# A hybrid decoder layer on one core: transposes of the normed rows move to the score banks, their inverse root comes from a square root, the last row blocks rank earlier, and one product gets its own bank

## Chip, core and metric

The kernel runs on one core of one Trainium2 chip. The metric is device microseconds for one execution. Times before the change: 1425.96, 1429.08 and 1431.47 us, median 1429.08 us. Engines are named as in the profile: PE (TensorE matmuls), PEld (its weight loads), DVE (VectorE), ACT (ScalarE), POOL (GpSimd), SP (SyncE, which issues most DMAs).

## The reference, cut to what matters

One layer over 1024 rows of 1024 columns, in float32:

```
proj = rms_norm(h, norm1_w) @ w_in
o_a  = gated delta rule, 4 heads      (scan over the rows)
o_b  = differential attention, 4 heads (two softmax maps per head)
h    = h + concat(o_a, o_b) @ w_out
u    = causal_dwconv3(rms_norm(h, norm2_w) @ w_up)      2 x 2816 columns: gate, up
h    = h + (silu(gate) * up) @ w_down
rms_norm(x, w) = x * rsqrt(mean(x*x) + 1e-6) * w
```

The change touches the passage from the attention to the third line from below: the output projection's second half, the second rms_norm, and the first products with w_up.

## The kernel before, in words

Every large product is made of three fp32r matmuls (high x high, high x low, low x high), so each operand is split into a high and a low part: ACT writes the high one, DVE or POOL the difference.

**Order of the work.** The kernel is written in the Tile framework: a list scheduler puts each engine's instructions in order when the program is built, by rank in the program. `part(name)` moves what it encloses ahead by `PRI[name]` places (lines 36 to 38). Each engine then runs its list strictly in order on the chip. Tiles come from rings: `g` (16 slots of 128x1024), `c` (4), `w` (5), `l` (2), `j` (2), and a new tile waits until the slot's last user is done.

**PSUM.** There are eight banks of 128x512. During the attention, pool `pq` has two banks of tag `G` (`psG`) and two of tag `t` (`sm`). Pool `pS2` (`psS`) has two tiles of two banks each, which hold the attention scores. After the attention both pools close (line 1201) and `pf[0]` and `pf[1]` take over, four banks each: `pf[0]` lies over `pq`'s four, `pf[1]` over the four score banks. `bank(i, s)` (line 1205) takes a bank of `pf[i % 2]`.

**The last head and the row blocks.** The 1024 rows are eight blocks of 128, and the last head's attention goes through them downwards, block 7 to block 0: scores and Exp in `attn1` (line 884; Exp in line 913), transposes `paT` and value products `pao` in `attn2` (line 924). `wout_b` (line 1107) follows block by block, in two steps:

- step 1 (`wb1`): load the rows into `hrow` (ring `c`), transpose the block's mixed heads into `trm` (`mix_T`, line 1048, one G bank), split it into `mhl` (lines 1054, 1055; ring `c`), 24 products into two `pwo` banks (lines 383 to 385), add them to `hrow` (line 1123), store it.
- step 2 (`wb2`): `rms_rows` (line 270) squares the row block with a sum on ACT (line 273, writing a fresh `g` tile `u`), takes the inverse root with `rsqrt_ss` (nine small DVE instructions, lines 193 to 198, the last six being three Newton rounds), and scales (line 276). `norm_T` (line 241) transposes `u` into two `sm` banks `tr` (line 246). `combine` (line 1069) reads them.

`combine` prepares a fast (Strassen-like) 2x2 block product: blocks 7 to 4 are split (lines 1085 to 1087). For blocks 3 to 0 ACT and DVE form `t1`, `t2`, `t3` and the splits of B22 and T2 (lines 1095 to 1104, line 1101 being the last read of the `tr` banks), POOL forms `t4` (line 1105).

**The first w_up products.** `up_early` (line 1246), for column blocks 0 and 1, computes two products that need only blocks 7 to 4 ("11" and "21", 24 matmuls each) into one bank `pe` of `pf[1]` (line 1254). Its weights hold four of the five `w` slots until they are done. `mv_split` (line 1211) splits T1, T3 and T4. `up(j)` (line 1261) makes the weight sums on POOL (lines 1270 to 1273), splits them (line 202 for rx, ry, rz) and runs five products of 12 matmuls in the order T2, T1, T3, 22, T4 (lines 1230 to 1232), in banks `pa` and `pc` of `pf[j % 2]`; for j from 2 on also "11" and "21". `rsqrt_act` (line 260) already exists: it is what the first stage of the kernel uses for its own norm, with Sqrt on ACT (line 264), then a reciprocal and one Newton round on DVE (lines 265 to 268).

Of the kernel before, what the change touches and what calls it, by code (L numbers as in the profile page):

```python
# [34 lines left out]

PRI = dict(dprep=1000, dscan=930, dinv=200, dout=100, dproj=100, dz1=100, qk0=370, v0=400,
           d_dec=0, d_k=-25, d_q=0, d_nat=50, d_sc=800, d_v=0, d_w=-430, qkn=970, qks=25, a2o=0,
           prep0=160, early_w=300, early=0, attn1=0, attn2=0, attn3=25, prep=-25, fill=0, wa=0, wb1=0, wb2=25, ffn=110)
FS = [2, 1, 2, 3, 2, 2, 2, 2]
PP0, PP1 = 4, 2  # L40
PRE_K = {5: 1, 6: 0}
# [17 lines left out]
def hybrid_layer(ctx, tc, x, positions, norm1_w, w_in, dn_conv_w, dn_a_log, dn_dt_bias,  # L59
# [60 lines left out]
    def psG(s="pG"):  # L120
        return pq.tile([P, 512], F32, tag="G", name=nm(s), bufs=2)
# [118 lines left out]

    def norm_T(src, ps_fn):
        pss = []
        for q in range(2):
            ps = ps_fn("tr")
            for k in range(4):
                PE.transpose(ps[:, k * P:(k + 1) * P], src[:, (4 * q + k) * P:(4 * q + k + 1) * P], ident)
            pss.append(ps)
        return pss
# [21 lines left out]
    def rms_rows(src, wrow, dst, junk, rsq=rsqrt_ss):  # L270

        ss = small("ss", 1, 4)
        S.activation(junk, src, AF.Square, accum_out=ss)
        rs = small("rs", 1, 4)
        rsq(ss, rs, D)
        V.scalar_tensor_tensor(dst, src, rs, wrow, op0=ALU.mult, op1=ALU.mult)
        return ss
# [769 lines left out]

    def mix_T(src, last):

        ps = psG("trm")  # L1050
        for k in range(4):
            PE.transpose(ps[:, k * P:(k + 1) * P], src[:, k * P:(k + 1) * P] if k < 3 else last, ident)
        hl = ct_("mhl", F32R)
        S.activation(hl[:, 0:512], ps, AF.Copy)
        V.tensor_tensor(hl[:, 512:1024], ps, hl[:, 0:512].bitcast(F32), op=ALU.subtract)
        return hl
# [12 lines left out]
    def combine(pss, u, tt):  # L1069

        o = slice(tt % 4 * P, tt % 4 * P + P)
        by = lambda ap: ap.rearrange("p (k t) -> p k t", t=P)
        if tt == NT - 1:
            mv_new("11")
            mv_new("21")
        if tt == 3:
            mv_new("22")
            mv_new("T2")
        if tt >= 4:
            if tt % 2 == 1:  # L1080
                stage[tt], stage[tt - 1] = ([gt("k1"), gt("k4")],) * 2
            half = slice(tt % 2 * 512, tt % 2 * 512 + 512)
            for q, name in enumerate(("11", "21")):
                hv, lv = (t[:, :, o] for t in stage[name])
                S.activation(hv, by(pss[q]), AF.Copy)
                V.tensor_tensor(lv, by(pss[q]), hv.bitcast(F32), op=ALU.subtract)
                S.activation(stage[tt][q][:, half], pss[q], AF.Copy)
            return
        b12, b22 = pss
        t1, t4 = (t[:, tt % 2 * 512:tt % 2 * 512 + 512] for t in stage[tt + 4])  # L1090
        t2 = u[:, 0:512]
        if tt % 2 == 1:
            stage["T3"] = stage.get("T3", []) + [gt("t3")]
        t3 = stage["T3"][-1][:, tt % 2 * 512:tt % 2 * 512 + 512]
        S.activation(t3, b12, AF.Copy)
        V.tensor_tensor(t1, b12, t1, op=ALU.subtract)
        V.tensor_tensor(t2, b22, t1, op=ALU.subtract)
        V.tensor_tensor(t3, b22, t3, op=ALU.subtract)
        hv, lv = (t[:, :, o] for t in stage["22"])
        S.activation(hv, by(b22), AF.Copy)  # L1100
        V.tensor_tensor(lv, by(b22), hv.bitcast(F32), op=ALU.subtract)
        hv, lv = (t[:, :, o] for t in stage["T2"])
        S.activation(hv, by(t2), AF.Copy)  # L1103
        V.tensor_tensor(lv, by(t2), hv.bitcast(F32), op=ALU.subtract)
        G.tensor_tensor(t4, t4, t2, op=ALU.subtract)

    def wout_b():

        w2row = gt("w2row")
        nc.scalar.dma_start(w2row, norm2_w.broadcast_to([P, D]))  # L1110
        spare = itertools.chain([ltr] * 2, [jtr], [wt], [gtr] * 4)
        wfs = [load_wo(4, c, G, lambda s: next(spare)(s)) for c in range(2)]

        def tile_(tt):
            rows = slice(tt * P, (tt + 1) * P)
            hrow = ct_("hrow")
            nc.sync.dma_start(hrow, hA_dram[rows, :])
            mb = jt("mb")
            nc.sync.dma_start(mb[:, 0:384], mix_dram[rows, :])
            hl = mix_T(mb, o3[tt])  # L1120
            for c in range(2):
                ps = mix_mm(hl, wfs[c])
                V.tensor_tensor(hrow[:, c * 512:(c + 1) * 512], ps, hrow[:, c * 512:(c + 1) * 512], op=ALU.add)
            nc.sync.dma_start(h_dram[rows, :], hrow)
            yield
            u = gt("u2")
            rms_rows(hrow, w2row, u, u)
            combine(norm_T(u, sm), u, tt)
            yield

        return [tile_(tt) for tt in reversed(range(NT))]
# [90 lines left out]
    def product(ps, w, name, start):  # L1222


        wh, wl = w
        xh, xl = mv[name]
        for k in range(4):
            ks = slice(k * P, (k + 1) * P)
            first = start and k == 0
            PE.matmul(ps, wh[:, ks], xh[k], start=first, stop=False, skip_group_check=not start)  # L1230
            PE.matmul(ps, wh[:, ks], xl[k], start=False, stop=False, skip_group_check=not start)  # L1231
            PE.matmul(ps, wl[:, ks], xh[k], start=False, stop=k == 3, skip_group_check=not start)  # L1232
# [28 lines left out]
    def up(j, early=None):  # L1261

        x_, y_, z_, w_ = raw_("rx"), raw_("ry"), raw_("rz"), lt("rw")
        gate, upc = j * P, (NF + j) * P
        load_half(w_, 0, upc, 8)
        load_half(x_[:, 512:1024], 0, gate)
        load_half(z_[:, 0:512], 4, gate)
        a21, a22, a11, a12 = w_[:, 0:512], w_[:, 512:1024], x_[:, 512:1024], z_[:, 0:512]
        s2, s1, s3, s4 = x_[:, 0:512], y_[:, 0:512], y_[:, 512:1024], z_[:, 512:1024]
        G.tensor_tensor(s1, a21, a22, op=ALU.add)  # L1270
        G.tensor_tensor(s2, s1, a11, op=ALU.subtract)  # L1271
        G.tensor_tensor(s3, a11, a21, op=ALU.subtract)
        G.tensor_tensor(s4, a12, s2, op=ALU.subtract)
        ws2, w11 = halves(split_w(x_))
        ws1, ws3 = halves(split_w(y_))
        w12, ws4 = halves(split_w(z_, None, T, jtr))
        wl_ = ltr("w22")
        w22 = (wl_[:, 0:512], wl_[:, 512:1024])
        S.activation(w22[0], a22, AF.Copy)
        V.tensor_tensor(w22[1], a22, w22[0].bitcast(F32), op=ALU.subtract)  # L1280
        add = lambda o, a, b: V.tensor_tensor(o, a, b, op=ALU.add)
        cg, cu = ct_("cg"), ct_("cu")
        x1 = cu[:, LAST] if early is None else early[:, 0:512]
        a, c = bank(j, "pa"), bank(j, "pc")
        product(a, ws2, "T2", True)
        if early is None:
            e = bank(j, "pe")
            product(e, w11, "11", True)
            S.activation(x1, e, AF.Copy)
        else:  # L1290
            G.tensor_copy(cg[:, LAST], early[:, 512:1024])
        product(c, ws1, "T1", True)
        add(cg[:, FIRST], a, x1)
        product(a, ws3, "T3", False)
        add(cu[:, FIRST], c, x1)
        if early is None:
            product(e, w12, "21", False)
            S.activation(cg[:, LAST], e, AF.Copy)
        add(cu[:, FIRST], a, cu[:, FIRST])
        product(c, ws4, "22", False)  # L1300
        add(cg[:, FIRST], c, cg[:, FIRST])
        product(a, w22, "T4", False)
        add(cu[:, LAST], a, x1)
        accs = []
        for part_, src in enumerate((cg, cu)):
            ct = part_ * NF + j
            acc = ct_("acc")
            S.activation(acc, src, AF.Identity, scale=fcw[:, 88 + ct:89 + ct], bias=fcw[:, 132 + ct:133 + ct])
            for sft in (1, 2):
                jj = 2 - sft  # L1310
                V.scalar_tensor_tensor(acc[:, sft:], src[:, :T - sft], fcw[:, jj * 44 + ct:jj * 44 + ct + 1],
                                       acc[:, sft:], op0=ALU.mult, op1=ALU.add)
            if part_ == 0:
                S.activation(acc, acc, AF.Silu)
            accs.append(acc)
        G.tensor_tensor(accs[1], accs[0], accs[1], op=ALU.mult)  # L1316
        nc.sync.dma_start(act_dram[j * P:(j + 1) * P, :], accs[1])
# [83 lines left out]
```

## Time and profile before

| | |
|---|---|
| three runs | 1425.96, 1429.08, 1431.47 us |
| the profiled execution | 1430.1 us, span 1428.4 us |
| PE busy | 1334.5 us, 93% of the span |
| DVE, ACT, POOL busy | 61%, 43%, 26% |
| last row blocks and start of w_up | about 676 to 780 us of the span |

A row of the timeline gives start, duration, engine, line, operation, output and inputs, count and, in brackets, how long the engine stood idle before it and what it waited for. Matmuls overlap, so PE's busy time counts a matmul's whole duration; the distance between starts is what one costs. "Granted clock" 1.00 is 2.4 GHz, 0.50 is 1.2 GHz.

### The profile page before, as it was taken

What the parts mean: (1) busy time and instruction counts of PE and PEld (TensorE: products, weight loads), DVE (VectorE), ACT (ScalarE), POOL (GpSimd) and SP (SyncE); (2) the same over time, 40 slices, a digit from 0 to 9 for tenths busy, and PEclk for the clock granted to TensorE, in tenths of its full rate; (3) what the DMA queues carried; (4) which work ended last, traced back from release to release, by engine and by line L of the source; (5) the groups of instructions that cost most, each with busy time, mean ns of one, the idle gap of its engine ahead of it and who ended that gap; (6) DMA issues with size and microseconds to landing.
All of it is one profiled execution on the core that took longest, in us unless ns stands there. A gap on an engine that the chain in (4) does not pass through costs nothing. (4 is left out here: it accounts for less than half of the span.)

```text
span 1428.4 us, 20608 instructions
## 1 busy us (share of the span) xinstructions
PE 1334.5 (93%) x7927; PEld 1126.6 (79%) x7927; DVE 878.3 (61%) x1745; ACT 611.3 (43%) x1086; POOL 377.0 (26%) x295
## 2 busy tenths in 40 slices
PE   7998898989989998999887999999999989999998
PEld 6876676888989986778665788888888868888887
DVE  5467978886342368867787666666666656334321
ACT  6445454533325365665554444444444435222220
POOL 3044313131242245240022434444333420000000
PEclk8999999999999999999998999999999999999999
DMA  7231112031543267455331222222222247547421
GB/s 225 83 80 35 34 39 75 17 113 66 162 109 116 88 169 192 105 134 162 123 121 29 89 74 89 85 78 89 89 74 82 82 137 243 195 149 229 139 88 59
DMA packets 143393, 155.14 MB, mean 109 GB/s; under 512 B 9279, under 2 KB 114367, under 8 KB 143295
## 3 DMA queue, kind: packets, MB, share of 16 engines
q1 hardware_dynamic: 130815, 144.14, 31.8%
q0 software_dynamic: 11008, 8.39, 3.1%
q8 instruction: 62, 1.02, 0.3%
q10 hardware_dynamic: 1472, 1.29, 0.3%
q14 instruction: 36, 0.29, 0.1%
HBM read 111.32 MB, written 38.29 MB: 105 GB/s over the span
## 5 line engine op out<-in xcount | busy, mean ns | idle before, releaser
L385 PE MATMUL pd<-whi,gl 128*128 128x512 f32 x352 | 137.0, 389 | 0.0
L383 PE MATMUL pd<-whi,gh 128*128 128x512 f32 x352 | 137.0, 389 | 0.0
L384 PE MATMUL pd<-wlo,gh 128*128 128x512 f32 x352 | 137.0, 389 | 0.0
L204 POOL TENSOR_TENSOR wlo<-raw,whi 128x1024 fp32r<-128x1024 f32 x34 | 83.8, 2471 | 194.1 <-PE gT L424 68.2
L1316 POOL TENSOR_TENSOR acc<-acc,acc 128x1024 f32<-128x1024 f32 x22 | 53.6, 2437 | 243.8 <-issue 215.5
L403 PE MATMUL pn<-whi,xn 128*128 128x256 f32 x448 | 116.3, 293 | 0.0
L404 PE MATMUL pn<-whi,xn 128*128 128x256 f32 x448 | 115.4, 291 | 0.0
L1339 ACT ACTIVATE gh<-act 128x1024 fp32r<-128x1024 f32 x42 | 44.6, 1061 | 123.9 <-PE pd L384 100.2
L1340 DVE TENSOR_TENSOR gl<-act,gh 128x1024 fp32r<-128x1024 f32 x42 | 52.0, 1241 | 68.9 <-ACT gh L1339 68.6
L403 PEld LDWEIGHTS pn<-whi,xn 128*128 128x128 f32 x448 | 87.3, 195 | 0.3
L404 PEld LDWEIGHTS pn<-whi,xn 128*128 128x128 f32 x448 | 87.0, 195 | 0.1
L202 ACT ACTIVATE whi<-raw 128x1024 fp32r<-128x1024 f32 x58 | 61.0, 1052 | 52.1 <-issue 18.3
L206 DVE TENSOR_TENSOR wlo<-rx,whi 128x1024 fp32r<-128x1024 f32 x22 | 28.9, 1315 | 82.6 <-ACT whi L202 82.3
L424 PE MATMUL gT<-xn,wlo 128*128 128x512 f32 x192 | 79.3, 413 | 0.0
L1230 PE MATMUL pa<-xT,whi 128*128 128x512 f32 x176 | 70.5, 400 | 9.3 <-ACT xT L1103 5.3
L422 PE MATMUL gT<-xn,whi 128*128 128x512 f32 x192 | 78.8, 410 | 0.0
L423 PE MATMUL gT<-xn,whi 128*128 128x512 f32 x192 | 78.6, 409 | 0.0
L202 ACT ACTIVATE whi<-rx 128x1024 fp32r<-128x1024 f32 x22 | 23.3, 1061 | 127.4 <-POOL rx L1271 127.4
L383 PEld LDWEIGHTS pd<-whi,gh 128*128 128x128 f32 x352 | 66.1, 188 | 13.8
L385 PEld LDWEIGHTS pd<-whi,gl 128*128 128x128 f32 x352 | 66.1, 188 | 13.7
L384 PEld LDWEIGHTS pd<-wlo,gh 128*128 128x128 f32 x352 | 66.1, 188 | 13.6
L206 DVE TENSOR_TENSOR wlo<-raw,whi 128x1024 fp32r<-128x1024 f32 x24 | 29.4, 1225 | 72.3 <-PE pd L384 53.1
(377 smaller groups left out, 3765.9 us busy)
## 6 DMA issues: line engine op xcount, KB each, us to landing
act<-act_dram SPq DMA_DIRECT2D x42, 512.0 KB, 4.5
rw<-in_w_up_dram SPq DMA_DIRECT2D x22, 512.0 KB, 3.8
act_dram<-acc SPq DMA_DIRECT2D x22, 512.0 KB, 2.6
raw<-in_w_down_dram SPq DMA_DIRECT2D x22, 512.0 KB, 4.4
raw<-in_w_in_dram SPq DMA_DIRECT2D x18, 512.0 KB, 4.0
pn_dram<-pn SPq DMA_DIRECT2D x16, 512.0 KB, 3.4
rx<-in_w_up_dram SPq DMA_DIRECT2D x22, 256.0 KB, 2.8
rz<-in_w_up_dram SPq DMA_DIRECT2D x22, 256.0 KB, 3.3
```

The costliest lines, as they stand in the source:

```text
L202: S.activation(hi, raw[:, 0:w], AF.Copy)
L204: G.tensor_tensor(lo, raw[:, 0:w], hi.bitcast(F32), op=ALU.subtract)
L206: V.tensor_tensor(lo, raw[:, 0:w], hi.bitcast(F32), op=ALU.subtract)
L383: PE.matmul(ps, lh, rh, start=first, stop=False)
L384: PE.matmul(ps, lh, rl, start=False, stop=False)
L385: PE.matmul(ps, ll, rh, start=False, stop=last)
L403: PE.matmul(o, xs(xn, 0, kt, a, b), wh, start=kt == 0, stop=False)
L404: PE.matmul(o, xs(xn, 1, kt, a, b), wh, start=False, stop=False)
L422: PE.matmul(o, whi[:, kt, :], xs(x_, 0, kt, *qs), start=kt == 0, stop=False)
L423: PE.matmul(o, whi[:, kt, :], xs(x_, 1, kt, *qs), start=False, stop=False)
L424: PE.matmul(o, wlo[:, kt, :], xs(x_, 0, kt, *qs), start=False, stop=kt == NK - 1)
L1230: PE.matmul(ps, wh[:, ks], xh[k], start=first, stop=False, skip_group_check=not start)
```

## The change

Four edits. `wb2` goes from 25 to 60 places. `norm_T` called without a bank function takes one score tile of two banks (`psS`) in place of two `sm` banks, and `mix_T` takes an `sm` bank in place of a G bank. `rms_rows` in step 2 uses `rsqrt_act`. In `up(0)` the product "22" moves from fourth to second place into a bank `pd` of its own, and one more add joins it to the result.

```diff
-           prep0=160, ... attn3=25, ... wb1=0, wb2=25, ffn=110)
+           prep0=160, ... attn3=25, ... wb1=0, wb2=60, ffn=110)
...
     def norm_T(src, ps_fn):
         pss = []
+        pair = psS("tr") if ps_fn is None else None
         for q in range(2):
-            ps = ps_fn("tr")
+            ps = pair[:, q * 512:(q + 1) * 512] if ps_fn is None else ps_fn("tr")
...
     def mix_T(src, last):
-        ps = psG("trm")
+        ps = sm("trm")
...
             u = gt("u2")
-            rms_rows(hrow, w2row, u, u)
-            combine(norm_T(u, sm), u, tt)
+            rms_rows(hrow, w2row, u, u, rsqrt_act)
+            combine(norm_T(u, None), u, tt)
...
         a, c = bank(j, "pa"), bank(j, "pc")
         product(a, ws2, "T2", True)
+        if j == 0:
+            d = bank(j, "pd")
+            product(d, ws4, "22", True)
...
         add(cu[:, FIRST], a, cu[:, FIRST])
-        product(c, ws4, "22", False)
+        if j == 0:
+            add(cg[:, FIRST], d, cg[:, FIRST])
+        else:
+            product(c, ws4, "22", False)
         add(cg[:, FIRST], c, cg[:, FIRST])
```

## Rows read from the trace of the kernel before

**Rows 1.** The page, part 1: busy time of each engine.
```profile
PE 1334.5 (93%) x7927; PEld 1126.6 (79%) x7927; DVE 878.3 (61%) x1745; ACT 611.3 (43%) x1086; POOL 377.0 (26%) x295
```
**Rows 2.** Stretches: length, PE, PEld, DVE, ACT, POOL busy (x), clock, DMA share, GB/s.
```profile
694.00:716.00 22.00, 16.47 (x90) 12.90 (x89) 16.59 (x61) 11.31 (x25) 0.00 (x0) 1.00 0.44 141
...
741.50:748.90 7.40, 7.32 (x24) 5.56 (x24) 6.58 (x16) 4.69 (x9) 2.09 (x2) 0.77 0.13 40
748.90:753.40 4.50, 0.00 (x0) 0.00 (x1) 4.36 (x6) 1.10 (x2) 2.46 (x2) 0.84 0.11 34
...
760.60:767.00 6.40, 5.55 (x15) 4.10 (x16) 6.40 (x10) 3.19 (x7) 0.45 (x1) 0.61 0.00 0
767.00:780.00 13.00, 13.00 (x59) 10.76 (x58) 8.91 (x11) 4.71 (x5) 0.00 (x0) 1.00 0.14 40
...
820.00:860.00 40.00, 40.00 (x177) 32.96 (x176) 25.70 (x28) 17.20 (x19) 15.67 (x11) 1.00 0.28 88
```
**Rows 3.** What PE waited for, 676 to 768 us: total us, times, longest.
```profile
PE tr L246 <- DVE u L276: 10.4, 5, 4.6
PE pa L1230 <- ACT xT L1103: 5.3, 1, 5.3
PE tr L246 <- DVE x L1101: 4.1, 1, 4.1
PE pa L1231 <- DVE xT L1104: 0.8, 1, 0.8
```
**Rows 4.** Timeline: PE's transposes of blocks 6 and 4 (first and last of three).
```profile
695.65 1.06 PE L246 MATMUL tr<-k_sb,u 128*128 128x128 f32 x8 [0.95 <-DVE u L276]
...
715.64 1.09 PE L246 MATMUL tr<-k_sb,u 128*128 128x128 f32 x8 [2.28 <-DVE u L276]
```
**Rows 5.** Timeline: block 5, end of the squares to the scaling, and the next split.
```profile
701.80 0.19 ACT L273 ACTIVATION_READ_ACCUMULATOR u<-hrow 128x1 f32 x1
...
704.42 1.28 DVE L276 SCALAR_TENSOR_TENSOR u<-hrow,rs,w2row 128x1024 f32<-128x1024 f32 x1
...
705.87 0.60 ACT L1054 ACTIVATE mhl<-trm 128x512 fp32r<-128x512 f32 x1 [3.89 <-DVE u L276]
```
**Rows 6.** Timeline: the first stage's inverse root by `rsqrt_act`, two blocks of it.
```profile
16.28 0.20 ACT L273 ACTIVATION_READ_ACCUMULATOR u<-x 128x1 f32 x1
...
17.49 1.28 DVE L276 SCALAR_TENSOR_TENSOR u<-x,rs,w1row 128x1024 f32<-128x1024 f32 x1
...
26.04 0.20 ACT L273 ACTIVATION_READ_ACCUMULATOR u<-x 128x1 f32 x1
...
29.87 1.28 DVE L276 SCALAR_TENSOR_TENSOR u<-x,rs,w1row 128x1024 f32<-128x1024 f32 x1
```
**Rows 7.** Timeline: squares of block 7, Exp of block 0; by line: a table load.
```profile
679.51 1.04 ACT L273 ACTIVATE u<-hrow 128x1024 f32<-128x1024 f32 x1
...
688.45 0.37 ACT L913 ACTIVATE p<-S,nmx 128x128 f32<-128x128 f32 x1
...
L1314 ACT ACT_TABLE_LOAD x1 | 1.3, 1283 | 0.0
```
**Rows 8.** Timeline: block 0 from its sum to the last read of its transposes.
```profile
734.74 0.68 DVE L1123 TENSOR_TENSOR hrow<-pwo,hrow 128x512 f32<-128x512 f32 x1
...
736.06 1.06 ACT L202 ACTIVATE whi<-rx 128x1024 fp32r<-128x1024 f32 x1 [3.78 <-POOL rx L1271]
...
740.79 0.20 ACT L273 ACTIVATION_READ_ACCUMULATOR u<-hrow 128x1 f32 x1
...
750.91 2.37 DVE L276 SCALAR_TENSOR_TENSOR u<-hrow,rs,w2row 128x1024 f32<-128x1024 f32 x1
...
756.12 1.06 ACT L202 ACTIVATE whi<-rx 128x1024 fp32r<-128x1024 f32 x1 [6.12 <-POOL rx L1271]
...
762.12 0.68 DVE L1101 TENSOR_TENSOR x<-tr,x 128x512 fp32r<-128x512 f32 x1
```
**Rows 9.** The early products: by tile (duration min/median/max, first and last start).
```profile
L1230 PE MATMUL pe<-x,whi x16: 387/392/673, 723.6 to 748.0; 128*128 128x512 f32 x16
```

More of the change, by code (lines that the diff above doesn't have):

```diff
@@ L37 @@
            d_dec=0, d_k=-25, d_q=0, d_nat=50, d_sc=800, d_v=0, d_w=-430, qkn=970, qks=25, a2o=0,
-           prep0=160, early_w=300, early=0, attn1=0, attn2=0, attn3=25, prep=-25, fill=0, wa=0, wb1=0, wb2=25, ffn=110)
+           prep0=160, early_w=300, early=0, attn1=0, attn2=0, attn3=25, prep=-25, fill=0, wa=0, wb1=0, wb2=60, ffn=110)
 FS = [2, 1, 2, 3, 2, 2, 2, 2]
```

## The prediction, made before the changed kernel was run

> **What bounds the kernel now.** I read the page's busy shares first [rows 1]: PE is busy 93% of the span, so time can only be won where PE stands still, or runs at the lower clock. Then the table of stretches [rows 2]: from 820 us on PE has no gap (40.00 of 40.00 us), while between 694 and 767 us, where the last head's attention passes over into the w_up products, it has several. The reader should see two gaps there, and that the clock falls to 0.61 and 0.77 after them. Third, the list of what PE waited for [rows 3]: 10.4 us for `u` ahead of the transposes, 4.1 us for a `tr` bank that line 1101 had not yet read, 5.3 and 0.8 us for T2: 20.6 us. The lower level of the clock adds a little. At full clock a matmul of 512 columns costs 40/177 = 0.226 us; in 741.50 to 748.90 it cost 7.40/24 = 0.308, in 760.60 to 767.00, less the 0.8 us wait, 5.6/15 = 0.373 [rows 2]. That is 24 x 0.082 + 15 x 0.147 = 4.2 us. In all some 25 us, 1.7% of the span, is the most that the whole passage could return.
>
> **The inverse root, blocks 6 to 4.** For block 5 it takes from 701.99 (end of the squares) to 704.42, 2.4 us, until the scaling starts [rows 5]. `rsqrt_act` in the first stage takes 1.0 us for the same step, from 16.48 to 17.49 [rows 6]. The gain is on the path: PE waits for `u` ahead of these transposes, 0.95 us for block 6 and about 2.3 us for each of blocks 5 and 4 [rows 4], and the next split `mhl` waits for the same `u` [rows 5], because it needs the `c` slot that `hrow` gives up then. So 1.4 us each for blocks 5 and 4, and at most 0.95 us for block 6: 3.7 us. Against it stands a table load of 1283 ns [rows 7] when Sqrt follows Exp. Bounds 2.5 and 3.7 us, I take 3.
>
> **Block 0's chain.** It decides the end of the passage. Before, line 1123 gives block 0's last sum at 735.42, the squares end at 740.99, the scaling starts at 750.91 and lasts 2.37 us, and line 1101 has read the last `tr` bank at 762.80 [rows 8]. I call that last time X. What moves it:
> - The three rounds above: 3 us (2.5 to 3.7).
> - Eleven of the 48 early products (`pe`, three groups of 16, from 723.6 us on [rows 9]) stand in PE's queue ahead of or between block 0's output products, 11 x 0.226 = 2.5 us. They go behind, for the reason in the next part.
> - The squares came 4.4 us after they could (740.99 - 735.42 less 1.2 us of their own), since ACT stood in its queue at `whi<-rx`, which waited for POOL [rows 8]. With 60 places in place of 25 they may pass it. Bounds 0 and 4.4; I take 3.
> - The root itself, 9.9 us because its nine small steps stand in DVE's list between splits of 0.7 to 1.3 us each. New: 1.0 to 3.6 us, the two blocks of rows 6, the second of which was also crowded. It saves 6.3 to 8.9; I take 7.5.
> - The scaling ran at nearly twice the 1.28 us of the same instruction elsewhere [rows 5, 8]: 0 to 1.1, I take 0.5.
> - ACT's first read of the transposes stood behind the next `whi<-rx` [rows 8], some 2.2 us: 0 to 2.2, I take 1.5.
>
> Sum 18 us, bounds 11.3 and 22.8: X = 744.8, between 740.0 and 751.5. DVE keeps X from falling further: it was full while PE waited (4.36 of 4.50 us, 6.40 of 6.40 [rows 2]) and the new root takes only five small steps of nine from it per block.
>
> **The price: the score banks.** `pf[1]` lies over the score banks, and `up_early` asks for a bank of `pf[1]`. Before, nothing had used these banks since the scores of block 0 (their Exp at 688.45 [rows 7]), and so the 48 early products could fill PE's gaps from 723.6 to 748.5 [rows 9]. Now `tr` stands there until X. I take it that a pool's banks are given out only when the last tile of the pool before it is released; then the 48 products start at X, and PE has next to nothing between block 0's sums and X. They take 48 x 0.226 = 10.8 us. PE then stands where it stood at 760.65, when T2 began, so the change in time is X + 10.8 - 760.65, less the 0.8 us wait inside T2, which the early products now cover: X - 750.65. With X = 744.8 that is 5.9 us faster, with the bounds 10.7 faster and 0.9 slower. PE starts again after a pause in both cases, so the lower clock costs about the same 2 us.
>
> **What comes to nothing.** The 4.1 us wait for a `tr` bank [rows 3] goes away, but it stood in a gap of PE that the early products no longer fill either; block 0's chain holds its effect. `trm` in `sm`: both `pwo` banks stay free for products, and attention's last `paT` and `pao` share two banks with `trm` where they shared them with `tr`. "22" second: 12 products that need no split of T1, T3 or T4 go first. PE had no wait from 767 to 780 us [rows 2], so nothing is won, but T1's low parts, which come late, get 2.7 us of cover. If that cover failed, the wait would be at most a few splits of 0.7 us. The extra add is another 0.7 us of DVE where it is busy 8.91 of 13.00 us [rows 2]. rx's low part waits for a `w` slot until the first early column block is done; the second column block, 24 x 0.226 = 5.4 us, covers that. No DMA is added.
>
> The table loads deserve a look against the notes. Block 7's squares (679.51) precede the last Exp (688.45) [rows 7]; all other Sqrt follow it. So Sqrt, Exp, Sqrt make three loads, 3.8 us of an ACT that is half busy. The Trainium skill ("ScalarE: Activation LUTs", section "Table sets: the hidden batching unit") says that Exp and Sqrt lie in different sets and are to be batched, at about 2.7 us a switch with a drain; by it these three would be about 8 us of ACT, an estimate, with the same place in the order.
>
> **The rivals.**
> 1. *The early products keep covering* (chance 0.15): banks come free one by one, when block 1's pair is read. For: each pool of the last stage has its waits by tile. Against: then the order between two pools sharing a bank would have to be known early. T2 would start 2.15 us before X as now, and X lies 2.5 us later: 745.1 in place of 760.65, 15.5 us earlier and 0.8 us less waiting, about 1413.
> 2. *The chain stays long* (0.18): ACT and DVE, each strictly in order, again put weight splits ahead of block 0, as at 736.06 and 756.12 [rows 8]. X is between 748 and 756: within 0.5%, about 1430.
> 3. *Slower: the cover is lost and the chain isn't shortened* (0.08). Place: PE between block 0's sums and X. Price: the 10.8 us of early products behind X. It decides above X = 750.65, and over 0.5% (7.1 us) above 757.8. With only the eleven products' 2.5 us won, X = 760.3 and the time is 1439.
> 4. *Every Sqrt pays two loads* (0.04): if the scheduler, with the blocks ranked earlier, put Exps between all eight, 16 loads of 1.283 us would be 20.5 us of ACT, mostly on the chain from squares to `u`: with 2.6 us per block it would eat the 1.4 us gain and add 1.2 us for each of eight blocks, some 10 us, 1439 or less. Against: only block 0's two Exps come after the first squares. This is what the Trainium skill's batching rule would warn of.
>
> **The numbers.** The sum is against the profiled execution, 1430.1 us, of which 1428.4 us is the span: 1430.1 - 5.9 = 1424.2 us. That execution is 1.0 us above the median 1429.08, so I forecast 1423 us, with an own range of 1418 to 1430 (chance 0.55). A measurement of this kernel can tell about 0.5%, 7.1 us, from no change. The forecast exceeds that when X is below 743.5, about half of its range: 0.28 faster, 0.27 same. With rival 1, faster is 0.43; same, with rival 2, is 0.45; slower, rivals 3 and 4, is 0.12. The range runs from rival 1's 1413 to 1432, which leaves out most of rivals 3 and 4 and the lower end of rival 1.
>
> **What would show it.** In the new profile: the last read of `tr` (line 1101) near 745 us; the first `pe` product after it, or, for rival 1, before it; a gap of PE of over 8 us between block 0's output products and `pe`, with few transposes in it; no wait of `tr` for line 1101; `u` about 1 us after the squares for blocks 6 to 4; three or four ACT_TABLE_LOADs more at most before 700 us; and PE without a gap from `pe` through "22". I am wrong if the first `pe` stands where it stood, if line 1101 ends after 751 us, or if the passage before 716 us didn't get shorter.

## The result, and the profile after

The changed kernel takes **1442.52 us** (median of 8 runs, 1436.68 to 1447.79) against 1429.53 us for the kernel before beside it (8 runs, 1425.15 to 1432.43): ratio **1.0092, interval 1.0068 to 1.0116**. The forecast was 1423 us with a range of 1413 to 1432. It is slower, by about 13 us.

The profiled execution of the changed kernel took 1437.84 us (span 1436.1 us), 7.7 us more than the one of before. It is the second fastest of its eight runs, so the traces show 7.7 of the 13 us; the rest is spread between runs, of which no trace was taken.

Stretches of the changed kernel, with the columns of [rows 2]:

```profile
736.90:749.70 12.80, 0.00 (x0) 0.00 (x0) 8.03 (x15) 5.08 (x8) 6.23 (x5) 0.59 0.20 68
749.70:756.40 6.70, 3.86 (x12) 2.66 (x13) 3.86 (x5) 1.79 (x3) 1.27 (x1) 0.50 0.23 66
756.40:770.00 13.60, 13.60 (x54) 10.81 (x53) 3.67 (x6) 5.74 (x10) 0.81 (x1) 0.88 0.07 20
...
780.00:820.00 40.00, 33.99 (x139) 26.47 (x138) 26.99 (x26) 17.44 (x18) 18.39 (x13) 0.96 0.26 79
```

PE's gaps of before ([rows 2] show one of them, from 748.90) have become one, of 12.8 us without a single matmul, and in the stretch behind it PE's granted clock is 0.50, the lower level. Where the early products went is shown by their tile, with the columns of [rows 9]:

```profile
L1231 PE MATMUL pe<-x,whi x16: 389/397/628, 756.4 to 769.2; 128*128 128x512 f32 x16
```

In [rows 9] they ran from 723.6 to 748.0. Now the first starts at 756.4, and line 1102 (1101 before) ends its last read of a `tr` bank at 756.34 in the timeline of block 0:

```profile
736.50 0.39 PE L386 MATMUL pwo<-whi,mhl 128*128 128x512 f32 x1
...
739.50 1.06 ACT L202 ACTIVATE whi<-rx 128x1024 fp32r<-128x1024 f32 x1 [3.47 <-POOL rx L1272]
...
741.94 1.06 ACT L202 ACTIVATE whi<-rz 128x1024 fp32r<-128x1024 f32 x1 [1.39 <-POOL rz L1274]
...
743.42 0.61 ACT L1104 ACTIVATE xT<-u 128x512 fp32r<-128x512 f32 x1
...
744.07 0.69 DVE L1105 TENSOR_TENSOR xT<-u,xT 128x512 fp32r<-128x512 f32 x1 [4.56 <-ACT xT L1104]
...
745.28 0.68 DVE L1124 TENSOR_TENSOR hrow<-pwo,hrow 128x512 f32<-128x512 f32 x1
...
746.96 0.19 ACT L274 ACTIVATION_READ_ACCUMULATOR u<-hrow 128x1 f32 x1
...
748.31 1.29 DVE L277 SCALAR_TENSOR_TENSOR u<-hrow,rs,w2row 128x1024 f32<-128x1024 f32 x1
...
749.75 1.94 PE L247 MATMUL tr<-k_sb,u 128*128 128x128 f32 x8 [12.86 <-DVE u L277]
...
755.66 0.68 DVE L1102 TENSOR_TENSOR x<-tr,x 128x512 fp32r<-128x512 f32 x1
```

That `pe` and X meet so closely isn't a wait. PE's own rows from T2's first product on:

```profile
754.49 0.80 PE L1231 MATMUL pa<-xT,whi 128*128 128x512 f32 x1 [2.80 <-ACT xT L1104]
755.08 0.77 PE L1231 MATMUL pd<-x,whi 128*128 128x512 f32 x1
755.79 0.80 PE L1232 MATMUL pa<-xT,whi 128*128 128x512 f32 x1
756.38 0.63 PE L1231 MATMUL pe<-x,whi 128*128 128x512 f32 x1
```

The first `pe` follows the matmul ahead of it after 0.59 us, as `pd` follows `pa`, and no wait is shown for it. What holds it is its place in PE's list, behind block 0's transposes and the first products of T2 and "22".

Now block 0's chain: read it upwards from the scaling at 748.31. From the end of the squares it takes 1.2 us, where [rows 8] has 9.9: the new root works. But block 0's last sum, whose product PE had finished at 736.9, comes at 745.28. DVE stood 4.56 us at block 1's `xT`, because ACT stood at two weight splits that waited for POOL.

What PE waited for (columns of [rows 3]), from 676 to 768 us in the changed kernel:

```profile
PE tr L247 <- DVE u L277: 13.1, 2, 12.9
PE pwo L384 <- ACT mhl L1055: 8.6, 5, 4.0
PE pa L1231 <- ACT xT L1104: 2.8, 1, 2.8
```

The wait of `pwo` for `mhl` was 0.7 us before. From 768 to 830 us the kernel before shows

```profile
PE pa L1230 <- DVE cg L1281: 1.9, 2, 1.7
PE pa L1230 <- DVE cu L1281: 1.1, 1, 1.1
PE pa L1232 <- DVE wlo L206: 0.6, 1, 0.6
```

and the changed kernel

```profile
PE pa L1231 <- DVE cg L1282: 3.7, 1, 3.7
PE pc L1233 <- DVE wlo L206: 1.7, 1, 1.7
PE pc L1231 <- DVE cu L1282: 1.5, 1, 1.5
PE pa L1233 <- DVE wlo L206: 0.6, 1, 0.6
PE pa L1231 <- DVE cu L1282: 0.2, 1, 0.2
```

7.7 us in place of 3.6. Most of this isn't the mark of the slower kernel, though: e1 below, as fast as the kernel before, has 6.8 us in the same window, with the same

```profile
PE pa L1231 <- DVE cg L1282: 3.7, 1, 3.7
PE pc L1231 <- DVE cu L1282: 1.5, 1, 1.5
```

but no wait of `pc` (T1) for `wlo`. Ahead of that 1.7 us stands a new wait of DVE (what DVE waited for, 736 to 770 us):

```profile
DVE wlo L206 <- PE pe L1232: 8.0, 1, 8.0
DVE xT L1105 <- ACT xT L1104: 4.6, 1, 4.6
...
```

The two early column blocks' weights hold four of the five `w` slots, the high part of `rx` the fifth. Its low part waits for the first early product group to be done, and the splits of T1, T3 and T4 stand behind it in DVE's list. In the kernel before that wait was 0.25 us.

### The profile page after: what moved, and what is told of

Same layout as the page of the kernel before. It is cut to its first block, busy times and chain, and to the rows that moved or that the text cites. A ratio compares the mean times of both kernels' runs of the same rounds, so it can differ in the third digit from the quotient of the medians.

```text
span 1436.1 us, 20552 instructions
## 1 busy us (share of the span) xinstructions
PE 1335.4 (93%) x7927; PEld 1126.5 (78%) x7927; DVE 875.3 (61%) x1706; ACT 615.9 (43%) x1097; POOL 375.3 (26%) x295
```

## The experiments

Ratios are to runs of the kernel before on the same chip. The table has, from each profiled execution, in us: the start of block 7's transposes (b7), of the last `pwo` product, of block 0's last sum and of the first T1 product (`pc`), X (end of block 0's last read of `tr`), and the first `w_down` product. There is one profiled execution of each kernel, and b7, which stands ahead of nearly all that the edits change, differs by up to 5 us between them. So times of two kernels are better compared from b7 on. T1's start has 12 more products ahead of it, 2.7 us, wherever "22" goes second: in all kernels but those marked *.

```
run                     median (runs)  ratio, interval            b7     pwo    sum    X      T1     down
before*                 1429.53 (8)    1                         684.8  732.5  734.7  762.8  766.9  1185.0
changed                 1442.52 (8)    1.0092 (1.0068, 1.0116)   685.7  736.5  745.3  756.3  773.8  1192.8
e1_banks_back           1430.85 (12)   1.0000 (0.9986, 1.0014)   686.4  735.3  736.9  757.9  765.3  1185.8
e2_banks_only*          1441.08 (6)    1.0070 (1.0051, 1.0089)   683.9  731.1  731.5  755.6  770.4  1193.0
e3_root_only*           1428.00 (12)   0.9981 (0.9964, 0.9997)   688.1  739.0  742.1  762.4  766.3  1186.6
e4_early_free_bank      1433.02 (12)   1.0015 (1.0000, 1.0031)   686.4  737.8  746.7  757.7  768.4  1188.1
e5_splits_after_block0  1437.15 (9)    1.0042 (1.0025, 1.0059)   688.6  740.2  744.3  755.6  772.3  1194.9
e6_splits_and_bank      1429.68 (12)   0.9993 (0.9981, 1.0005)   688.0  739.2  743.3  754.7  766.0  1186.5
e7_trm_back             1437.94 (6)    1.0052 (1.0034, 1.0070)   683.6  733.8  734.6  752.3  770.1  1190.8
e8_both_and_trm_back    1423.86 (6)    0.9954 (0.9936, 0.9972)   688.7  740.2  740.7  754.0  760.7  1181.6
e9_root_one_load*       1426.77 (11)   0.9982 (0.9968, 0.9996)   685.5  733.1  736.2  756.5  760.2  1180.4
e10_bank_and_trm        1428.21 (12)   0.9993 (0.9980, 1.0007)   684.6  735.7  736.2  753.5  758.7  1179.6
e11_first_splits_only   1424.68 (11)   0.9967 (0.9955, 0.9979)   683.9  735.2  735.7  749.1  755.8  1175.9
e12_all_and_one_load    1425.96 (12)   0.9976 (0.9960, 0.9991)   685.5  741.1  741.6  754.9  761.6  1185.5
e13_before_no_early*    1435.19 (12)   1.0038 (1.0022, 1.0055)   685.4  733.7  735.7  762.6  768.7  1188.0
e14_after_no_early      1435.80 (12)   1.0041 (1.0024, 1.0059)   687.1  738.3  747.2  763.0  771.1  1188.9
e15_after_one_early     1438.68 (6)    1.0062 (1.0038, 1.0086)   688.8  740.4  749.0  761.2  773.0  1198.2
```

**Which part costs the time.** e1 puts the banks back in the changed kernel:

```
-        ps = sm("trm")
+        ps = psG("trm")
...
-            combine(norm_T(u, None), u, tt)
+            combine(norm_T(u, sm), u, tt)
```

> The changed kernel with its banks put back: tr in sm and trm in psG as before, while the square root, 60 places and the separate bank of 22 stay. Theory A (the lost cover decides: 48 early products of 10.8 us stand behind block 0's transposes): the early products start before 745 us again, PE's gap of 12.9 us before the last transposes is filled, and the time falls by 8 to 12 us from 1442.5, to 1430 to 1434, ratio to before 1.000 to 1.004. Rival B (the table loads of Sqrt and Exp make the rounds longer): no bank matters, the time stays at 1440 or more, ratio 1.007 or more, with the 3 loads still there. Rival C (60 places or the moved 22 spoil the order of the splits): stays above 1.007 too.

1.0000: the whole loss is gone, and with it the `mhl` waits (0.7 us). The three loads are still there. e2 is the opposite, the kernel before with `tr` as a pair from `psS`, passed as `None`, and `trm` from `sm`:

> The kernel before with only the two bank moves (tr as a pair in a score bank, trm in sm); root, places and 22 as before. Theory A: X, the last read of block 0's tr, stays near 760 since eleven early products go behind but nothing shortens the chain; all 48 early products come after X; the time is X - 750.65 = 8 to 12 us over before, ratio 1.006 to 1.009, which is all of the change's loss or more. Rival B (table loads): no Sqrt here, so no loss, ratio 0.998 to 1.002. Rival C (60 places, 22): no loss either.

1.0070: the bank move by itself costs about what the change costs. Its X is 755.6, not near 760. All early products start after it (755.7). Its PE waits from 768 to 830 us have the low weights at their head:

```profile
PE pc L1233 <- DVE wlo L206: 4.2, 1, 4.2
```

e3 adds only `rsqrt_act` to the call of `rms_rows`:

> The kernel before with only rsqrt_act in place of rsqrt_ss in the last stage. Theory A: the early products keep their cover, the root is shorter, X falls by some 0 to 8 us, of which little reaches the end because the early products and the weight splits are in the way: ratio 0.995 to 1.000. Rival B: three table loads and a later Exp make the rounds 7 to 4 longer by some 3 us or more each time PE waits: ratio 1.002 to 1.006. Rival C: as Theory A, 0.995 to 1.000.

0.9981: as Theory A had it, hardly a gain. Rival B is out as the cause of the loss, though one of its loads does stand on PE's way at block 6 (shown further down).

**Is it the cover?** e4 changes one number in the changed kernel:

```
-        e = bank(1, "pe")
+        e = bank(0, "pe")
```

> The changed kernel with one edit: the early products ask for a bank of pf[0] in place of pf[1]. pf[0] lies over the banks of trm and pwo, which are free once block 0's output products are summed (738.8 and 746.0 in the changed kernel), while tr stays in the score banks. Theory A: some 20 of the 48 early products go into PE's gap of 12.9 us ahead of the last transposes, the others behind; the clock falls less; the time is 4 to 10 us below the changed kernel, 1433 to 1438, ratio to before 1.002 to 1.006. Rival B and C: the gap wasn't the cost, the time stays at 1442, ratio 1.008 or more.

1.0015, 9.5 us below the changed kernel's median, at the low edge of what was expected. The first early product starts at 737.99. Only 8 run ahead of block 0's transposes, where PE still waits 11.2 us for `u`; but the others start right behind them, at 752.7, and so ahead of X, which is no sooner (757.7). T1 starts 5.4 us sooner than in the changed kernel.

**Block 0's chain.** e5 delays the weight splits of column blocks 0 and 1 (for `rx`, `ry`, `rz` and `w22`). `gate` is block 0's sum of squares:

```
+        if gate is not None:
+            S.activation(hi[:, 0:1], gate, AF.Copy)
         S.activation(hi, raw[:, 0:w], AF.Copy)
```

> The changed kernel with the weight splits of the first two column blocks made to wait (by a one-column ACT copy of block 0's sum of squares into each high part) until block 0's squares are done, so that ACT no longer stands at whi<-rx and whi<-rz with block 1's xT, and through it block 0's last sum, queued behind. The early products stay where the change put them, behind X. Theory A (in-order lists held block 0's chain, and the end moves with X): block 0's last sum comes at about 740 in place of 745.3, X at about 750.5 in place of 756.3, and the time falls by about 6 us from 1442, to 1435 to 1438, ratio to before 1.003 to 1.006. Rival (weight splits themselves are what PE waits for after X): the splits come later, the waits for wlo at 776 grow by what X gains, ratio stays 1.007 or more.

The time is as expected (1.0042), the trace only in part: the last sum comes at 744.26, not 740. ACT's wait is now

```profile
741.98 0.63 ACT L1106 ACTIVATE xT<-u 128x512 fp32r<-128x512 f32 x1 [2.29 <-DVE u L1100]
```

so with the weight splits out of ACT's way DVE's own list, with the reads of blocks 2 and 1 ahead of block 0's sum, sets it. This execution was late by 3.0 us already at block 7's transposes (688.64 against 685.66); counted from there, X is 66.95 us away in place of 70.68, 3.7 us sooner, not 6. And PE now waits 5.3 us for the second block's `whi` after 768, a cost of the edit itself. e6 is e4 and e5 together:

> Both edits: early products in a bank of pf[0] and the weight splits behind block 0's squares. Theory A: PE's gap ahead of the last transposes shrinks from 11.2 us to some 5, T2 starts 4 to 7 us sooner than with the free bank alone: 1427 to 1430, ratio to before 0.997 to 1.000. Rival: the gain is lost again in waits for wlo after 768, ratio 1.001 to 1.003 as with the free bank alone.

0.9993, in the band of Theory A. T2 and T1 start 2.4 us sooner than in e4, 4.0 us counted from b7, the low end of what was expected; the same 5 us wait for `whi` is in it. e7 takes only `trm` back to `psG`:

> The changed kernel with only trm back in psG, tr stays in the score banks. It prices the half of the bank move that takes trm into sm, beside paT and pao: the five waits of pwo for mhl (8.6 us, before 0.7) should go. Theory A (block 0's transposes and the 48 products behind them decide): block 0's chain gains little, ratio 1.006 to 1.009 as the changed kernel. Rival (the late mhl makes every round longer, and that is the loss): the time falls by 4 to 8 us, ratio 1.001 to 1.004.

1.0052 lies between the two bands. The `mhl` waits hardly fell (8.6 to 6.6 us), so the expected mechanism failed. What changed is block 0's last sum, which now follows its product at once:

```profile
734.57 0.68 DVE L1124 TENSOR_TENSOR hrow<-pwo,hrow 128x512 f32<-128x512 f32 x1
...
751.57 0.68 DVE L1102 TENSOR_TENSOR x<-tr,x 128x512 fp32r<-128x512 f32 x1
```

X is 4.1 us sooner, but b7 is 2.1 us sooner too, so at most 2.0 us are the edit's; the profiled time falls by the same 2.0 us, the median by 4.6. This fits the forecast's rule that the end moves with X, in one pair of executions. The sum itself came 10.7 us sooner: from there to the scaling it now takes 9.7 us in place of 3.0, with weight splits ahead of the squares in ACT's list and ahead of the root in DVE's. e8 joins all three edits:

> The edits of e6 and trm back in psG: 20 early products stand ahead of the last transposes in PE's list. If the pieces add up: e6 less what e7 wins, 1424 to 1429, ratio to before 0.995 to 0.999. If PE has all its cover already: as e6.

0.9954: **faster than both kernels**, 7 us below the one before. PE waits 1.0 us for `u` ahead of the last transposes, where the changed kernel has 12.9.

**Parts of that version, and the table loads.** e10 is e8 without the delayed splits, e11 delays them for the first column block alone, e12 is e11 with `rsqrt_ss` kept for blocks 7 and 6; e9 is the kernel before with the new root for blocks 5 to 0.

> The changed kernel with the early products in pf[0] and trm back in psG, without the waiting of the weight splits. 30 early products stand ahead of the last transposes. If the held-back splits gave e8 its time: 1428 to 1431, ratio to before 0.998 to 1.000. If the banks alone did: 1422 to 1426, ratio 0.994 to 0.997.

0.9993: the banks alone bring the changed kernel back to before, and the delayed splits bring the rest. In this kernel PE hardly waits for `u` ahead of the last transposes (0.3 us), but it waits 4.3 us for ACT to copy an early product out of its bank (`early`), before the next one can be added there.

> As e8, but only the first column block's weight splits wait for block 0's squares; the second's are free again, which in e5 and e6 let PE wait 5.2 us for whi after 780. If that wait is what the held-back splits cost: 1421 to 1424, ratio 0.993 to 0.996. If it is taken up elsewhere: as e8, 0.995.

0.9967, the same as e8 within the intervals. X is the earliest of all, 749.1, but counted from b7 it is where e8 has it (65.1 and 65.3 us), and in both PE then waits 4.0 us for `wlo`.

> The kernel before with rsqrt_act for blocks 5 to 0 only; blocks 7 and 6 keep rsqrt_ss, so that every Sqrt follows the last Exp and one ACT_TABLE_LOAD stands where the root for all blocks had three. Theory A (the loads stand on ACT beside other work; what the root saves is held by the waits behind it): ratio to before 0.996 to 1.000, as with the root for all blocks (0.998). Rival B (three loads and the later Exp of block 0 cost 2 to 4 us of PE at 690 to 700): 2 to 4 us below the root for all blocks, 1424 to 1426, ratio 0.993 to 0.996.

> As e11, with rsqrt_ss kept for blocks 7 and 6, so that one table load is left of three. Theory A: as e11 within 2 us. Rival B (the loads cost PE time at 690 to 700): 2 to 4 us below e11.

e9 is 0.9982 beside e3's 0.9981, e12 1.3 us above e11: the 2 to 4 us that Rival B asked of one load for three aren't there. Both edits also give blocks 7 and 6 the longer root back, so a small gain could hide behind that.

**What the early products cost where they now stand.** e13, e14 and e15 change one number (`EARLY = 2` to 0, 0 and 1). The computation is the same; the products are made later, in their column blocks.

> The kernel before with no early products (EARLY = 0): the first two column blocks make their 11 and 21 products in place, as all the others do. Theory A (the cover is what the bank move takes away): the 48 products leave PE's gaps at 724 to 748 empty; they come to 10.8 us, so the time rises by 6 to 11 us, 1436 to 1441, ratio 1.004 to 1.008, nearly as the bank move alone (1.007). Rival (the early products are worth nothing, the bank move costs by another way): ratio 0.998 to 1.002.

> The changed kernel with no early products. Theory A: nothing stood in the gap before block 0's transposes anyway, so nothing is lost, and the two weight pairs no longer hold w slots until PE comes to them: the 8 us wait of DVE at wlo<-rx goes and the waits for wlo after 768 with it, 2 to 5 us faster than the changed kernel, 1437 to 1440, ratio to before 1.005 to 1.008, and no slower than e13. Rival (the bank move costs by another way than the early products): as much above e13 as the changed kernel is above the kernel before, 9 to 13 us, 1448 or more.

> The changed kernel with one early column block in place of two, so that two of five w slots are held until X in place of four. Theory A: DVE's wait at wlo<-rx goes, 24 products stand behind X: 1 to 5 us faster than the changed kernel, 1437.5 to 1441, ratio 1.005 to 1.008. Rival (the slots don't matter): as the changed kernel, 1442, 1.008 to 1.010.

The kernel before loses 4.2 us without its early products, less than the 6 to 11 expected; the changed kernel *gains* 6.7 us, more than the 2 to 5 expected, and the two then stand within 0.6 us of each other. So without early products the whole change costs nothing that is clear of noise; a small loss by the bank move itself could still hide behind what the new root gains (0.9981 in e3). In e14 X comes later than in the changed kernel, 763.0, and still it is faster. The 8 us wait of DVE is gone, and this is all that PE waits for from 768 to 830 us:

```profile
PE pa L1231 <- DVE cu L1282: 0.4, 1, 0.4
```

e15 lies between, as expected. DVE's wait for a slot is gone in it too, but 2.1 us of PE's waiting for `wlo` at T1 stay, so the slots are not all of it (its profiled execution, 1443.4 us, was its slowest).

## Why the prediction was wrong, point by point

**The price of the score banks: the place right, the reason not.** The early products did go behind block 0's chain, and the change in time followed them: undoing the banks (e1), giving the products another bank (e4) or having none (e14) takes 11.7, 9.5 and 6.7 us back. This was rival 3's place and price, which the text held for the least likely but one. Its condition was met too, since X came at 756.3, above 750.65, for which the forecast's formula gives 5.7 us of loss; the traces have 7.7, the medians 13.

The reason given was that a pool's banks are given out only when the last tile of the pool before it is released. The traces speak against it. In the changed kernel the first `pe` shows no wait for X, and in e15 it starts at 762.07, 0.9 us behind X, again without a wait. In e4

```profile
737.99 0.39 PE L1231 MATMUL pe<-x,whi 128*128 128x512 f32 x1
...
746.66 0.68 DVE L1124 TENSOR_TENSOR hrow<-pwo,hrow 128x512 f32<-128x512 f32 x1
```

`pf[0]` gives a bank out 8.7 us before block 0's last `pwo`, in the pool under it, is read. So there banks come free one by one, as rival 1 had it. What made the early products late is their place in PE's list, and the pool that they ask for a bank decides that place (e4 changed nothing else). The place of the loss was forecast rightly, but by a reason that doesn't hold, so in part by luck. Why a bank of `pf[1]` puts them behind block 0's transposes, and which score bank `pe` got, no trace shows.

**X is the step that failed: 756.3 in place of 744.8.** Two of the forecast's own signs of being wrong came true: line 1101 ended after 751 us, and the rounds got no shorter. The miss splits into four terms:
- *The rounds and the eleven products* were to bring the last `pwo` from 732.5 to 727.0. It started at 736.5: 9.5 us missed, 0.9 of which b7 already has. The rounds got no shorter in any run with the new root; in e9, without extra loads ahead of block 5, the way from b7 to the last `pwo` is 47.6 us, as before (47.8). Of the 3 us taken for blocks 6 to 4, e3 shows what became: PE's waits for `u` are 2.4, 1.1 and 2.2 us where [rows 4] have 0.95, about 2.3 and 2.28.

```profile
696.78 1.28 ACT L264 ACT_TABLE_LOAD   x1
...
700.48 1.49 PE L246 MATMUL tr<-k_sb,u 128*128 128x128 f32 x8 [2.40 <-DVE u L276]
...
710.96 1.06 PE L246 MATMUL tr<-k_sb,u 128*128 128x128 f32 x8 [1.12 <-DVE u L276]
...
720.57 1.18 PE L246 MATMUL tr<-k_sb,u 128*128 128x128 f32 x8 [2.19 <-DVE u L276]
```

At block 5 the root saves 1.2 us of the 1.4 forecast; at block 6 a table load stands between the squares and the Sqrt, and the wait is 1.4 us longer; at block 4 the Sqrt stands in ACT's list behind another block's squares, and nearly nothing is saved. In the changed kernel PE hardly waits for `u` there, but the split `mhl` is late instead, 8.6 us. The text said what waits for `u` besides PE, but priced no new wait.

- *From the last `pwo` to the last sum* I had left 2.2 us as they were. It became 8.8: 6.6 us missed. Rival 2 named the cause, weight splits ahead of block 0 in ACT's list; e5 and e7 show DVE's list as well as ACT's behind it.
- *From the sum to the scaling* 5.7 us were forecast, 3.0 came: the root and the squares did better than their terms, by 2.7 us.
- *From the scaling to X* 9.9 were forecast, 8.0 came, 1.9 us better.

9.5 + 6.6 - 2.7 - 1.9 = 11.5 us. These terms aren't independent: e7 takes the second away, and more than half of it comes back in the third. The terms were right or too low where a step's own instructions got shorter and nothing new stood ahead of them; they failed where they took over the old order of the lists, because every edit made a new order. The bank move alone shows it: I took 2.5 us for its eleven products, and e2, with the old root, has X 7.2 us earlier (6.3 from b7), which nothing here divides between the products and the moved banks.

**What was priced at nothing and was not: the `w` slots.** "The second column block covers that" counted PE's time and not DVE's, which stood 8.0 us. T1 starts 6.9 us later than before, 4.2 without the moved 12 products; from there to the first `w_down` product another 3.6 us are lost (419.0 us with 12 products fewer, against 418.1), where I had none. In e2 the two are 3.6 and 4.4 us. Together 7.8 and 8.0, what the profiled executions show. What the slots cost in this is at most PE's wait for `wlo` right behind T1's start: 1.7 us here, and 4.2 in e2, where "22" doesn't stand ahead of T1 (e4, where DVE waits only 0.5 us for the slot, still has 1.0). The rest of the part behind T1 isn't the bank move's: e1 takes 420.5 us from T1 to `w_down`, more than the changed kernel, and ends where the kernel before ends. In e14 all these waits go, but there the 48 products also stand in their column blocks again, where they give PE work while DVE goes through its list; that the slots alone did it isn't shown.

**The cover was worth less than its products.** 10.8 us of matmuls filled the gaps; without them the kernel before loses 4.2 (e13). PE then waits only 0.8 us after 768 in place of 3.6, which is 2.8 of the 6.6 us between; the rest stays open. Every kernel that reaches T1 sooner gives some of it back like this: e1 starts T1 1.6 us sooner with 12 more products done, so 4.3 us sooner, and ends where it ended.

**What came to nothing at the end, as forecast:** "22" second and the 60 places (e1 against e3: 1.0000 and 0.9981, no difference clear of noise), and the table loads. There were three of 1.28 us, as in the forecast's order; the first stands at 681.86, the others here:

```profile
690.77 1.28 ACT L914 ACT_TABLE_LOAD   x1
692.06 0.37 ACT L914 ACTIVATE p<-S,nmx 128x128 f32<-128x128 f32 x1
...
693.05 1.05 ACT L274 ACTIVATE u<-hrow 128x1024 f32<-128x1024 f32 x1
...
694.09 0.59 ACT L1055 ACTIVATE mhl<-trm 128x512 fp32r<-128x512 f32 x1
...
694.70 1.28 ACT L265 ACT_TABLE_LOAD   x1
...
694.73 0.73 PE L384 MATMUL pwo<-whi,mhl 128*128 128x512 f32 x1 [3.98 <-ACT mhl L1055]
```

The second does stand on the way to a late `mhl` here, and e3 has one on the path at block 6, but e9 and e12 show that taking two out isn't felt at the end. In the changed kernel the instruction behind a load starts 0.01 us after it: the Exp at 692.06, the Sqrt at 695.99. So a switch takes ACT 1.3 us. The Trainium skill ("ScalarE: Activation LUTs", section "Table sets: the hidden batching unit") has about 2.7 us for a switch; this trace doesn't agree.

**Open.** Why the median of the changed kernel lies 4.7 us above its profiled execution; why `mhl` is late in every kernel with `tr` in the score banks (4.0 us in e2, 6.6 in e7, 8.6 in the changed kernel) and not with `tr` in `sm` (0.7 in e1 and e3). In the rows above it stands in ACT's list behind the Exps and the squares (693.05, 694.09); no run changed only that order.

## What to carry to other kernels

Banks that nothing uses in a stage may still be what the next stage starts on: before moving a tile there, look for what is laid over them, and give work that is meant to fill gaps a bank that comes free first (e4, one number, took back 9.5 us). Filling work that comes too late can be worse than none (e14): ask not only for its time, but what it holds and what stands behind it. A wait that is new in the slow kernel isn't yet its cause: look whether a kernel as fast as the old one has it too (e1). And where engines work through fixed lists, a chain can't be summed from the old trace by its parts: price each part's own instructions, and give what stands between them a range as wide as the longest wait next to it.

## What the runs showed of the hardware

Nothing new in kind. In its gap of 12.8 us PE's granted clock was 0.59 on average, and 0.50, the lower of its two levels, in the 6.7 us behind it; the first seven early products took 0.63 us apiece in place of 0.39, and started 0.43 us apart in place of 0.23.
